# A GDN / short-conv / differential-attention backbone on one core: moving activation tiles that begin off the 64-byte grid

## The chip, the cores and the metric

The kernel runs on one core of one Trainium2 chip. The metric is the device time of one execution in microseconds. Before the change it is 2574.88 us, the median of three runs (2573.0 to 2578.13).

## The reference

Two streams of 256 tokens of width 1024, a context and a latent stream, pass through four layers. A layer is a token mixer and a squared-ReLU MLP, each on a normalised and modulated input and added back through a gate:

```
h = rmsnorm(x) * (1 + scale) + shift      # shift, scale, gate: silu(c) @ ada_w[i] + ada_b[i]
x = x + gate1 * mixer(h)                  # layer 0, 3: gated DeltaNet; 1: short conv; 2: differential attention
x = x + gate2 * (square(relu(h2 @ w1)) @ w2)   # w1 1024 x 4096, w2 4096 x 1024
```

Both streams use the same weights; the last layer computes the latent stream alone after its mixer. The output is the latent stream after a last RMSNorm. All of it is float32, and the result must be that of float32 products.

## The kernel before, in words

**Products.** Activations stand transposed: 128 features on the partitions, 512 token columns (context, then latent) along them, eight such tiles for a width of 1024. A float32 product is made of three products in the fast float32 format (F32R): a weight block W is split into `whi` (rounded) and `wlo` (the rest), an activation tile into a high and a low part, and `prod` (L776) adds whi x high, whi x low and wlo x high into one PSUM bank. In each matmul the 128 x 128 weight block is the stationary operand and the activation tile streams past it as the moving operand; a weight load (PEld in the profile) stands ahead of every matmul and runs while the matmul before it streams. So the order for one k is: load whi, stream high; load whi, stream low; load wlo, stream high.

**Tiles.** `hh0..7` and `hl0..7` (L768, names hh and hl in the profile) are the high and low parts of the modulated input of a mixer or an MLP; `u00..u03`, `u10..u13` (L889, named u) are the two parts of 512 hidden features of the MLP, with two buffers each; `yh`, `yl` and the `y` tiles are the mixers' outputs on their way into the output projection. Weights arrive as `raw` (three buffers, SP's DMA queue, `pump_raw` L453), ACT casts them to `whi` and DVE (in the DeltaNet layers POOL) subtracts to get `wlo`; four pairs are held. The second weight of an MLP's last round is kept in pairs of its own, `whix` and `wlox`.

**Where they stand.** Every tile gets its place in a partition of the SBUF from the pools in order of request. As the program is built, `raw`, `whi`, `wlo`, h and u begin at multiples of 64 bytes. What the prediction uses is the distance in bytes, modulo 256, from the weight block that is loaded during a matmul to the tile that streams in it (a column half of 256 tokens, 1024 bytes on, changes nothing in it):

| moving tile | weight loaded meanwhile | distance mod 256 before |
|---|---|---|
| hh, hl | whi, wlo | 0 |
| u | whi, wlo | 128 |
| u | whix, wlox | 0 |
| yh, yl (layer 1) | whi, wlo | 128 |
| yh, yl (layer 1) | whix, wlox | 0 |
| y (layers 0 and 3) | whi, wlo | 32, in their last round 128 |
| y (layer 2) | whi, wlo | 224 |

**Order.** A recording planner (class `Issue`, L68) writes the order of the instructions of every engine: strands of work with priorities, each operation with a cost, and an estimate of when operands and buffers come free, by eighths of a tile's row (`buckets`, L131). PE's order is then fixed. In an MLP (L875 on) PE does, for each 512 hidden features f, the four blocks of w1 on h (24 matmuls each) and then the eight blocks of w2 on the u of f-1 (12 each): 96 and 96 matmuls that follow each other without other work between. The conv mixer does 20 blocks of 24 one after another. In the DeltaNet and attention mixers the blocks on h are interleaved with the small matmuls and transposes of the heads.

**Modulation rows of the next layer.** During the MLPs of layers 0 to 2 the strand `ada_rows` (L589) makes the 6 x 1024 modulation values of the next layer on DVE: 48 loads of 512 KB (`adat`, four buffers, three fetched ahead) over SP's queue, which carries the weights too, and two dot products (L281) for each.

Of the kernel before, what the change touches and what calls it, by code (L numbers as in the profile page):

```python
# [10 lines left out]
F32 = mybir.dt.float32  # L11
F32R = mybir.dt.float32r
# [8 lines left out]
P = 128  # L21
D = 1024
NCH = D // P
T = 256
TT = 2 * T
# [372 lines left out]
class Net:  # L398
# [3 lines left out]
    MM = 3  # L402
    HP, DHP = -20, -20
    SHARE = 0.7
    RAW = 3
    RINGS = (dict(u=4, kt=2, E=2, qd=1, NT=2, scr=2, Z=3, gate=2, o=3, NY=1),
             dict(u=4, kt=3, E=3, qd=3, NT=3, scr=3, Z=4, gate=4, o=4, NY=1))
# [45 lines left out]
    def pump_raw(self):  # L453
        while self.wraw < len(self.wlist):
            ap, kc, cols = self.wlist[self.wraw]
            if cols < P:
                r = self.I.tile(self.wp, "rawab", [P, kc, cols])
            elif sum(c >= P for _, _, c in self.wlist[self.wsplit:self.wraw]) < self.RAW:
                r = self.I.tile(self.wp, "raw", [P, kc, cols], F32, self.RAW)
            else:  # L460
# [119 lines left out]
    def ada_prio(self):  # L580


        self.ada_task.prio = 900 if self.ada_q < 8 + self.phase * self.SHARE else 5000

# [4 lines left out]
    def ada_rows(self, i, pool, ev):  # L589


        I, todo, raws = self.I, deque(range(48)), deque()
        mod = self.mods[i] = I.tile(self.sp, "mod", [P, 48, 2], F32, 2)
        s = I.tile(pool, "adas", [P, 2, D])
        I.load(s, self.a["cvb"])

        def fetch():
            if todo:
                w = I.tile(pool, "adat", [P, D], F32, 4)
                I.load(w, self.a["ada_wT"][i - 1, todo.popleft()])  # L600
                raws.append(w)

        for _ in range(3):
            fetch()
        for r in range(2):
            yield I.act(s[:, r, :], s[:, r, :], AF.Silu)
        I.table(AF.Exp)
        for m in range(48):
            w = raws.popleft()
            for r in range(2):  # L610
                junk = I.tile(pool, "adaj", [P, D], BF16)
                yield I.dot(mod[:, m, r:r + 1], junk, w, s[:, r, :], self.ada_b[:, i, m:m + 1])
            fetch()
            self.ada_ev[i][m // 2].on = m % 2 == 1
        ev.on = True
# [148 lines left out]
    def norm_start(self, i, which, st, halves=(0, 1)):  # L764
        I = self.I
        h = ([], [])
        for k in range(NCH):
            h[0].append(I.tile(self.sp, f"hh{k}", [P, TT], F32R))  # L768
            h[1].append(I.tile(self.sp, f"hl{k}", [P, TT], F32R))
        st["hev"] = [Event(), Event()]  # L770
        st["h"] = h
        for half in halves:
            I.spawn(self.norm_strand(i, which, st, half, h), 3 + half)
# [101 lines left out]
    def mlp(self, i, t0, st, nst, pl):  # L875
        I = self.I
        halves = [h for h in range(2) if h * T >= t0]
        cols = self.full(t0)
        h = st["h"]
        first = yield from self.joint(pl[0, 0], h, [HALF[x] for x in halves])  # L880
        with self.tc.tile_pool(name=f"mlp{i}", bufs=1) as up:
            us = {}
            self.wpool = up
            ada = Event(i + 1 == self.depth)
            if not ada.on:
                I.spawn(self.ada_rows(i + 1, up, ada), 5000)

            def u_tiles(f):
                us[f] = tuple([I.tile(up, f"u{x}{m}", [P, TT], F32R, 2) for m in range(4)] for x in range(2))  # L889

            def u_fin(f, m, ps):
                yield [lambda: I.slot(up, "r", 2)]
                r = I.tile(up, "r", [P, TT], F32, 2, True)
                u = I.tile(up, "u", [P, TT], F32, 2, True)
                yield I.act(r[:, cols], ps[:, cols], AF.Relu)
                I.rel(ps)
                yield I.act(us[f][0][m][:, cols], r[:, cols], AF.Square)
                yield I.act(u[:, cols], r[:, cols], AF.Square)
                yield I.vtt(us[f][1][m][:, cols], u[:, cols], us[f][0][m][:, cols].bitcast(F32), ALU.subtract)
                I.rel(r, u)  # L900

            nf = FF // 512
            for f in range(nf):
                u_tiles(f)
                if f == 0:
                    yield from self.joint_end(*first, lambda m, ps: I.spawn(u_fin(0, m, ps), 2))
                for m in range(0 if f else 4, 4):
                    yield [self.mm_slot()]
                    ps = self.mm_ps()
                    yield from self.block(pl[0, f][m], h, NCH, cols, ps)  # L910
                    self.done(pl[0, f][m])
                    I.spawn(u_fin(f, m, ps), 2)
                if f:
                    yield from self.proj_rounds(i, pl[1, f - 1], 4, 2, us.pop(f - 1), t0, 40, None)
            if i + 1 < self.depth:
                self.norm_start(i + 1, 0, nst)
            yield from self.proj_rounds(i, pl[1, nf - 1], 4, 2, us.pop(nf - 1), t0, 40, nst)
            self.wpool = None
            yield [ada]
# [890 lines left out]
```

## Time and profile before

| | |
|---|---|
| median of three runs | 2574.88 us |
| the profiled execution, its own time | 2573.83 us |
| its span, first to last instruction | 2572.1 us |
| PE busy | 2508.0 us (98%), 16396 matmuls |
| DVE, ACT, POOL busy | 1846.5 us (72%), 1252.0 us (49%), 389.1 us (15%) |
| granted TensorE clock, mean | 0.991 |

The profile has one line per group of instructions: the line of the kernel, the engine, what is written from what, the count, the busy time and the mean duration. A matmul's duration there runs to the end of its drain, while the next one has long begun: the time that a matmul costs its engine is the distance from its start to the next start, which the timeline gives and which is called the pitch here. Start times are us from the span's first instruction.

### The profile page before, as it was taken

Reading aid. Unit: us, or ns where it says so; the run is one execution under the profiler, and the core shown is the slowest. Engines: PE = TensorE matmul, PEld = TensorE weight load, DVE = VectorE, ACT = ScalarE, POOL = GpSimd, SP = SyncE. Lnnn points to the kernel's source line nnn. Section 1 sums busy time; section 2 is a strip of 40 time slices with the busy share of each in tenths; the row PEclk is TensorE's granted clock in tenths of the full one; section 3 lists DMA queues with packets and bytes.
Section 4 is the critical chain, followed back from the end, with each engine's and each line's share of the span. In section 5 each row is a group of like instructions: output and inputs, shape, how many; then the busy total and the mean of one; then the engine's idle time right before and its main releaser. Section 6 shows DMA issues by size and latency. Waiting matters only on the chain. (4 is left out here: it accounts for less than half of the span.)

```text
span 2572.1 us, 41962 instructions
## 1 busy us (share of the span) xinstructions
PE 2508.0 (98%) x16396; PEld 2090.8 (81%) x16396; DVE 1846.5 (72%) x3481; ACT 1252.0 (49%) x2349; POOL 389.1 (15%) x273
## 2 busy tenths in 40 slices
PE   7999999999999999999999999999999999997998
PEld 3778777888888988988889677888888978897998
DVE  5776776699955644999746666799965687775666
ACT  4665665543333433533243454543333577775554
POOL 0444544200000000000000000000000155463000
PEclk9999999999999999999999999999999999998999
DMA  7222212466634133566432322366634111122564
GB/s 290 91 67 67 91 58 75 156 220 213 220 98 125 60 97 107 197 207 219 148 94 77 95 66 70 115 213 215 210 115 124 51 59 42 50 68 75 172 184 129
DMA packets 91638, 323.30 MB, mean 126 GB/s; under 512 B 10288, under 2 KB 13872, under 8 KB 91056
## 3 DMA queue, kind: packets, MB, share of 16 engines
q1 hardware_dynamic: 91440, 320.62, 38.6%
q8 instruction: 129, 2.11, 0.3%
q14 instruction: 69, 0.57, 0.1%
HBM read 317.44 MB, written 1.05 MB: 124 GB/s over the span
## 5 line engine op out<-in xcount | busy, mean ns | idle before, releaser
L257 ACT CAST whi<-raw 128x1024 fp32r<-128x1024 f32 x380 | 399.5, 1051 | 796.4 <-PE ch L236 423.0
L274 DVE TENSOR_TENSOR wlo<-raw,whi 128x1024 fp32r<-128x1024 f32 x305 | 376.2, 1234 | 228.7 <-ACT whi L257 217.3
L236 PE MATMUL mm<-hh,whi 128*128 128x512 f32 (+1 forms) x1344 | 489.6, 364 | 0.0
L236 PE MATMUL mm<-hh,wlo 128*128 128x512 f32 (+1 forms) x1344 | 488.0, 363 | 0.9 <-DVE wlo L274 0.9
L236 PE MATMUL mm<-hl,whi 128*128 128x512 f32 (+1 forms) x1344 | 487.9, 363 | 0.0
L281 DVE CUSTOM_DVE_ANT_0 adaj<-adat,adas,pack 128x1024 bf16<-128x1024 f32 x288 | 368.7, 1280 | 9.4 <-ACT adas L253 5.7
L236 PE MATMUL ch<-u,whi 128*128 128x512 f32 (+1 forms) x1024 | 287.2, 367 | 0.0
L236 PE MATMUL ch<-hh,whi 128*128 128x512 f32 (+3 forms) x784 | 281.2, 359 | 2.1 <-ACT hh L253 2.1
L236 PE MATMUL ch<-hl,whi 128*128 128x512 f32 (+3 forms) x784 | 280.8, 358 | 0.9 <-DVE hl L277 0.9
L236 PEld LDWEIGHTS mm<-hh,wlo 128*128 128x128 f32 x1344 | 256.1, 191 | 31.2 <-issue 5.2
L236 PE MATMUL ch<-hh,wlo 128*128 128x512 f32 (+3 forms) x784 | 281.1, 359 | 0.0
L236 PEld LDWEIGHTS mm<-hh,whi 128*128 128x128 f32 x1344 | 256.4, 191 | 29.1 <-issue 3.7
L236 PEld LDWEIGHTS mm<-hl,whi 128*128 128x128 f32 x1344 | 256.4, 191 | 27.3 <-issue 3.0
L300 POOL TENSOR_TENSOR wlo<-raw,whi 128x1024 fp32r<-128x1024 f32 x75 | 183.2, 2444 | 220.3 <-ACT whi L257 141.0
L236 PE MATMUL mm<-u,whi 128*128 128x512 f32 (+1 forms) x768 | 215.5, 367 | 0.0
L236 PEld LDWEIGHTS ch<-u,whi 128*128 128x128 f32 x1024 | 183.5, 188 | 34.8
L236 PEld LDWEIGHTS <-Z 128*128 128x128 f16 x3072 | 147.3, 97 | 78.0 <-issue 43.9
L236 PE MATMUL ch<-u,wlo 128*128 128x512 f32 (+1 forms) x512 | 187.7, 367 | 0.0
L236 PE MATMUL ch<-Z 128*128 128x64 f16 (+1 forms) x2816 | 174.6, 199 | 7.7 <-DVE Z L269 3.3
L300 POOL TENSOR_TENSOR qk<-qk,rope 128x512 f32<-128x512 f32 x8 | 14.0, 1750 | 1099.6 <-DMA rt<-qk 1063.6
L277 DVE SCALAR_TENSOR_TENSOR x<-mm,mod,x 128x256 f32<-128x256 f32 x284 | 129.1, 479 | 66.6 <-PE mm L236 66.2
L269 DVE CAST_PREDICATED Z<-lev,ch 128x256 f16<-128x256 uint8 x384 | 144.4, 426 | 42.0 <-PE ch L236 38.8
(257 smaller groups left out, 4559.0 us busy)
## 6 DMA issues: line engine op xcount, KB each, us to landing
raw<-in_mlp_w SPq DMA_DIRECT2D x256, 512.0 KB, 3.6
adat<-in_ada_wT SPq DMA_DIRECT2D x144, 512.0 KB, 4.5
raw<-in_gdn_w_in SPq DMA_DIRECT2D x64, 512.0 KB, 3.6
adaw<-in_ada_w SPq DMA_DIRECT2D x48, 512.0 KB, 4.6
raw<-in_sconv_w_in SPq DMA_DIRECT2D x24, 512.0 KB, 3.6
raw<-in_diff_w_in SPq DMA_DIRECT2D x24, 512.0 KB, 3.8
raw<-in_gdn_w_out SPq DMA_DIRECT2D x16, 512.0 KB, 3.5
raw<-in_sconv_w_out SPq DMA_DIRECT2D x8, 512.0 KB, 3.6
```

Of the source, the lines that this page charges most:

```text
L236: op = Op("PE", c, [out], [lhsT, rhs], lambda: self.nc.tensor.matmul(out, lhsT=lhsT, rhs=rhs, start=start, stop=stop, **k), LAT["PE"])
L257: lambda: self.nc.scalar.copy(out=out, in_=in_), LAT["ACT"])
L269: op = self.vec(self._n(data), 130, [out], [data], lambda: self.nc.vector.copy_predicated(out=out, mask=mask, data=data))
L274: return self.vec(self._n(in0), 68, [out], [in0, in1], lambda: self.nc.vector.tensor_tensor(out=out, in0=in0, in1=in1, op=op))
L277: return self.vec(self._n(in0), 130, [out], [in0, in1, scalar], lambda: self.nc.vector.scalar_tensor_tensor(out=out, in0=in0, scalar=scala ...
L281: return self.vec(self._n(in0), 130, [out, junk], [in0, in1, init], lambda: self.nc.vector.tensor_tensor_reduce(out=junk, in0=in0, in1=in1 ...
L300: lambda: self.nc.gpsimd.tensor_tensor(out=out, in0=in0, in1=in1, op=op))
```

## The change

The eight hh and eight hl tiles and the u tiles become 528 instead of 512 columns long (2112 instead of 2048 bytes), and the 512 columns in use begin at a column offset of their own: 4, 8, 12 or 2 columns (16, 32, 48, 8 bytes) for the h tiles, four tiles each, and 1, 3, 5, 6 (high parts) and 7, 9, 10, 14 columns (low parts) for u, which is 4 to 56 bytes. As the tiles follow each other at 2112 bytes, the distance modulo 256 also turns by 64 from one h tile to the next. In the program as built the sixteen h tiles stand at sixteen different distances modulo 256 from the weights (hh: 16, 144, 32, 160, 48, 176, 8, 136; hl: 80, 208, 96, 224, 112, 240, 72, 200), and the u tiles at 132, 12, 148, 24, 156, 36, 168, 56, their second buffers 64 further on. The y, yh and yl tiles and all weights keep their distances. The planner's eighths of an h tile's row are 66 columns then, so that the two halves of a row share one of them. To make room the loads of the modulation rows have three buffers instead of four.

```diff
--- before.py
+++ after.py
@@ -402,6 +402,7 @@
     MM = 3
     HP, DHP = -20, -20
     SHARE = 0.7
+    UO = (1, 3, 5, 6, 7, 9, 10, 14)
     RAW = 3
     RINGS = (dict(u=4, kt=2, E=2, qd=1, NT=2, scr=2, Z=3, gate=2, o=3, NY=1),
              dict(u=4, kt=3, E=3, qd=3, NT=3, scr=3, Z=4, gate=4, o=4, NY=1))
@@ -596,7 +597,7 @@
 
         def fetch():
             if todo:
-                w = I.tile(pool, "adat", [P, D], F32, 4)
+                w = I.tile(pool, "adat", [P, D], F32, 3)
                 I.load(w, self.a["ada_wT"][i - 1, todo.popleft()])
                 raws.append(w)
 
@@ -765,8 +766,9 @@
         I = self.I
         h = ([], [])
         for k in range(NCH):
-            h[0].append(I.tile(self.sp, f"hh{k}", [P, TT], F32R))
-            h[1].append(I.tile(self.sp, f"hl{k}", [P, TT], F32R))
+            for x in range(2):
+                o = (4, 8, 12, 2)[(2 * k + x) // 4]
+                h[x].append(I.tile(self.sp, f"h{'hl'[x]}{k}", [P, TT + 16], F32R)[:, o:o + TT])
         st["hev"] = [Event(), Event()]
         st["h"] = h
         for half in halves:
@@ -886,7 +888,8 @@
                 I.spawn(self.ada_rows(i + 1, up, ada), 5000)
 
             def u_tiles(f):
-                us[f] = tuple([I.tile(up, f"u{x}{m}", [P, TT], F32R, 2) for m in range(4)] for x in range(2))
+                us[f] = tuple([I.tile(up, f"u{x}{m}", [P, TT + 16], F32R, 2)[:, self.UO[4 * x + m]:self.UO[4 * x + m] + TT]
+                               for m in range(4)] for x in range(2))
 
             def u_fin(f, m, ps):
                 yield [lambda: I.slot(up, "r", 2)]
```

PE's order stays as it was but for two swaps at the first layer's start. What moves are the loads and dot products of the modulation rows. On SP's queue, at the start of the first MLP (adat: modulation rows, raw: weights; in brackets the semaphores an issue waits for), there stand before:

```order
L323 DMA adat_6611<-in_ada_wT 128x1024
L323 DMA adat_6617<-in_ada_wT 128x1024 [waits DMAHW5_49,DMAHW1_49,DVE_49]
L323 DMA adat_6639<-in_ada_wT 128x1024 [waits DMAHW6_49,DMAHW2_49,DVE_49]
L323 DMA raw_6655<-in_mlp_w 128x1024 [waits DMAHW3_49,DVE_49]
L323 DMA raw_6693<-in_mlp_w 128x1024 [waits DMAHW4_49,DVE_49]
L323 DMA raw_6712<-in_mlp_w 128x1024 [waits DVE_49]
L323 DMA adat_6730<-in_ada_wT 128x1024 [waits DMAHW7_49]
L323 DMA raw_6742<-in_mlp_w 128x1024 [waits DMAHW3_49,DVE_49]
```

and now:

```order
L323 DMA adat_6611<-in_ada_wT 128x1024 [waits DMAHW5_49,DVE_49]
L323 DMA adat_6617<-in_ada_wT 128x1024 [waits DMAHW6_49,DMAHW1_49,DVE_49]
L323 DMA adat_6625<-in_ada_wT 128x1024 [waits DMAHW7_49,DMAHW2_49,DVE_49]
L323 DMA raw_6662<-in_mlp_w 128x1024 [waits DMAHW3_49,DVE_49]
L323 DMA adat_6679<-in_ada_wT 128x1024 [waits DMAHW4_49,DMAHW0_49,DVE_49]
L323 DMA raw_6700<-in_mlp_w 128x1024 [waits DVE_49]
L323 DMA raw_6719<-in_mlp_w 128x1024 [waits DVE_49]
L323 DMA raw_6737<-in_mlp_w 128x1024 [waits DMAHW3_49,DVE_49]
```

Each adat load now waits for DVE, and a raw load stands behind it more often: the load that fills a buffer follows the two dot products that have just emptied it, where the fourth buffer had been free for the time of a tile. On DVE, in the same place (ISA adaj: a dot product; wlo: a weight's low part; u: a hidden tile's low part), there stand before:

```order
L274 TENSOR_TENSOR wlo_6632<-raw_6261,whi_6631 128x1024
L281 ISA adaj_6641,mod_6586<-adat_6611,adas_6587,pack_85 128x1024
L281 ISA mod_6586 128x1
L274 TENSOR_TENSOR wlo_6658<-raw_6311,whi_6657 128x1024
L274 TENSOR_TENSOR u_1308_6599<-u_6635,u_1304_6595 128x512
L274 TENSOR_TENSOR wlo_6696<-raw_6349,whi_6695 128x1024
L274 TENSOR_TENSOR u_1309_6600<-u_6651,u_1305_6596 128x512
L281 ISA adaj_6672,mod_6586<-adat_6611,adas_6587,pack_85 128x1024
L281 ISA mod_6586 128x1
```

and now:

```order
L281 ISA adaj_6627,mod_6586<-adat_6611,adas_6587,pack_85 128x1024
L281 ISA mod_6586 128x1
L274 TENSOR_TENSOR wlo_6636<-raw_6261,whi_6635 128x1024
L281 ISA adaj_6646,mod_6586<-adat_6611,adas_6587,pack_85 128x1024
L281 ISA mod_6586 128x1
L274 TENSOR_TENSOR wlo_6665<-raw_6311,whi_6664 128x1024
L274 TENSOR_TENSOR u_1308_6599<-u_6639,u_1304_6595 128x512
L274 TENSOR_TENSOR wlo_6703<-raw_6349,whi_6702 128x1024
L274 TENSOR_TENSOR u_1309_6600<-u_6653,u_1305_6596 128x512
```

One more dot product stands ahead of a weight's low part; the work is the same, and the dot products of a layer keep their number, 96.

## Rows read from the trace of the kernel before

**Rows 1.** The page, parts 1 and 2: busy time, granted clock in 40 slices.
```profile
PE 2508.0 (98%) x16396; PEld 2090.8 (81%) x16396; DVE 1846.5 (72%) x3481; ACT 1252.0 (49%) x2349; POOL 389.1 (15%) x273
...
PEclk9999999999999999999999999999999999998999
```

**Rows 2.** Groups of matmuls by form: line, engine, names, tile, count, busy us, mean ns.
```profile
L236 PE MATMUL mm<-hh,whi 128*128 128x512 f32 x824 | 338.6, 411 | 0.0
...
L236 PE MATMUL ch<-u,whi 128*128 128x512 f32 x768 | 241.2, 395 | 0.0
...
L236 PE MATMUL ch<-hh,whi 128*128 128x512 f32 x536 | 208.9, 390 | 0.0
...
L236 PE MATMUL mm<-u,whi 128*128 128x512 f32 x576 | 180.9, 395 | 0.0
...
L236 PE MATMUL mm<-hh,whi 128*128 128x256 f32 x520 | 151.1, 290 | 0.0
...
L236 PE MATMUL ch<-hh,whi 128*128 128x256 f32 x224 | 64.3, 287 | 2.1 <-ACT hh L253 2.1
...
L236 PE MATMUL ch<-u,whix 128*128 128x256 f32 x280 | 51.9, 285 | 0.0
...
L236 PE MATMUL mm<-u,whix 128*128 128x256 f32 x168 | 30.5, 283 | 0.0
```

**Rows 3.** Timeline of PE in the first MLP: start us, length us, line, names, count.
```profile
562.72 0.39 PE L236 MATMUL mm<-hh,whi 128*128 128x512 f32 x1
...
584.50 0.40 PE L236 MATMUL ch<-u,whi 128*128 128x512 f32 x1
...
606.89 0.39 PE L236 MATMUL ch<-hh,whi 128*128 128x512 f32 x1
```

**Rows 4.** Stretches of one kind of matmul: from:to, length us, PE busy (count), clock, DMA.
```profile
874.62:983.45 108.83, 108.83 (x482) 1.00 0.36 111
998.16:1012.09 13.93, 13.93 (x61) 1.00 0.35 107
1624.74:1630.57 5.83, 5.83 (x27) 1.00 0.29 88
1630.80:1643.94 13.14, 13.14 (x112) 1.00 0.14 41
2400.46:2411.85 11.39, 11.39 (x98) 1.00 0.72 223
2411.85:2423.35 11.50, 11.50 (x98) 1.00 0.59 184
```

**Rows 5.** Timeline of PE at the start of the attention layer.
```profile
1415.36 0.40 PE L236 MATMUL ch<-hh,whi 128*128 128x512 f32 x1
...
1415.59 0.40 PE L236 MATMUL ch<-hl,whi 128*128 128x512 f32 x1
...
1415.83 0.39 PE L236 MATMUL ch<-hh,wlo 128*128 128x512 f32 x1
...
1416.52 0.60 PE L244 MATMUL ch<-ident,qk 128*128 128x128 f32 x4
...
1417.19 0.40 PE L236 MATMUL ch<-hh,whi 128*128 128x512 f32 x1
...
1419.26 0.39 PE L236 MATMUL ch<-hh,whi 128*128 128x512 f32 x1
```

**Rows 6.** Timeline of PE in the first DeltaNet layer.
```profile
119.52 0.38 PE L236 MATMUL ch<-abg,selb 96*128 96x512 bf16 x1
119.74 0.27 PE L236 MATMUL ch<-u 128*128 128x128 f32 x1
```

**Rows 7.** Waits: engine, what waited, for what: us in total, times, longest us.
```profile
ACT whi L257 <- PE ch L236: 423.0, 137, 9.0
...
ACT whi L257 <- PE mm L236: 330.2, 130, 4.5
```

**Rows 8.** The page, parts 5 and 6: the dot products of modulation rows, their loads.
```profile
L281 DVE CUSTOM_DVE_ANT_0 adaj<-adat,adas,pack 128x1024 bf16<-128x1024 f32 x288 | 368.7, 1280 | 9.4 <-ACT adas L253 5.7
...
adat<-in_ada_wT SPq DMA_DIRECT2D x144, 512.0 KB, 4.5
```


## The prediction

> **What bounds the kernel.** First the page: PE is busy 98% of the span, at 90% of the full clock or more in all slices but one [rows 1]. So the time is what PE's instructions cost one after another, and the questions are whether the change moves their pitch (start to next start), and whether it makes PE wait. Next the groups by form, for the counts: of the 512-column matmuls on h there are 824 and 536 in the whi-by-hh groups, and as many for hl and for wlo, 3 x 1360 = 4080; on u 768 and 576, and half as many for wlo, 2016; of 256 columns 3 x (520 + 224) = 2232 on h, and 1.5 x (280 + 168) = 672 on u with whix or wlox [rows 2]; the last MLP adds 7 x 96 = 672 on u with whi. The means there run to the end of the drain and are no pitch. So third the timeline and stretches of one kind of matmul. The counts in the stretches include one or two matmuls that were running when they began (and in one case the one that follows); the divisors here are those that start inside, by the code.
>
> In the first MLP 96 matmuls on h take 584.50 - 562.72 = 21.78 us, 226.9 ns each, and the 96 on u that follow 606.89 - 584.50 = 22.39 us, 233.2 ns [rows 3]: the same form, clock and neighbours, and 6.3 ns apart. The table of distances has h at 0 and u at 128 bytes (mod 256) from the weights that are loaded meanwhile. In the conv mixer, h again: 480 in 108.83 us, 226.7 ns. The yh and yl of that layer, at 128: 60 in 13.93 us, 232.2. The y of the attention layer, at 224, that is 32 bytes off the 64-byte grid: 25 in 5.83 us, 233.2 [rows 4]. So of 512 columns one kind stands out, at 227, and all others lie at 232 to 233. With 256 columns it is the other way round: h at distance 0 takes 11.50 us / 96 = 119.8 ns, u at 128 takes 11.39 / 96 = 118.6, y at 224 takes 13.14 / 111 = 118.4 [rows 4].
>
> h itself is not always at 227. Where other matmuls come between, at the start of the attention layer, five starts take 1416.52 - 1415.36 = 1.16 us, 232 each, and nine after the transposes 1419.26 - 1417.19 = 2.07 us, 230 [rows 5]. I read this as a rhythm: a row of matmuls at one distance, 0, settles after some matmuls into a pitch in which loads and streams hinder each other least at 512 columns (and somewhat more than elsewhere at 256). Why that is so no row shows.
>
> **The change part by part.** Its own part is the distances. Sixteen h tiles at sixteen distances, used in turn, leave no row of matmuls at one distance, and none at 0. I expect h to leave its 227 and to run at what all other distances show.
>
> h, 512 columns. Undisturbed are three MLPs of 7 x 4 blocks of 24, 2016, and the conv mixer's 480; of the 1584 others, among head work, I let 300 be settled. 2800 x (232.2 - 226.8) = +15.1 us. The rest already runs at 230 to 232: nothing.
>
> u, 512 columns. 2016 x (232.2 - 233.2) = -2.0 us: one mixed rhythm for another.
>
> h, 256 columns. 2232 x (118.5 - 119.8) = -2.9 us. u with whix and wlox stands at distance 0 too; at h's pitch, 672 x -1.3 = -0.9 us. u with whi in the last MLP is at 118.6 already: nothing.
>
> The sum is +9.3 us. Bounds of the new pitch, which no row shows for starts of 4 to 28 bytes off the grid: from below the nearest row is the bf16 matmul of 512 columns, 119.74 - 119.52 = 0.22 us [rows 6], half the bytes; at 220 for 512 columns and 110 for 256, h wins 2800 x 6.8 + 1280 x 11 = 33 us, u 2016 x 13.2 = 27, the 256-column ones 2904 x 9.8 + 672 x 8.6 = 34: -94 us. From above the longest regular pitch is the 1415.83 - 1415.59 = 0.24 us among the unsettled ones [rows 5]: 2800 x 13.2 + 1280 x 9 + 2016 x 6.8 = +62 us. I take 232.2 and 118.5 because three kinds of tile at three distances, one of them off the grid, agree within 1 ns.
>
> Three buffers instead of four for the modulation rows. 144 loads of 512 KB land 4.5 us after issue, 288 dot products take 1.28 us each [rows 8]. A load now waits on SP's queue for the dot products that have just been issued, and behind it stand loads of weights, which so come up to 2 x 1.28 = 2.6 us later. What hides it: ACT's cast of a weight block waits for PE to release an old pair 137 + 130 times, 423.0 + 330.2 us in all, 2.8 us a time [rows 7]; in these waits the raw weights lie ready. The dots have slack as well: 48 tiles in the seven rounds of 44.2 us that rows 3 show for an MLP, 309 us, are one in 6.4 us, and a load that is fetched two tiles ahead has 12.8 us for its 4.5. Nothing, then; if the cover were gone, up to 144 x 2.6 us is at stake.
>
> Writes to h and u at odd columns are on ACT (49%) and DVE (72%) [rows 1]; PE's wait for the first h of a block totals 2.1 us in its group [rows 2]. Nothing. The swaps at PE's start trade places of neighbours: nothing.
>
> The profiled execution took 2573.83 us, so 2583.1 by its own time; the median of the three runs lies 1.05 above it: 2584.
>
> **Two rules against the rows.** h and u in rows 3 and two kinds of 256 columns in rows 4 differ by 6.3 and 1.2 ns with nothing to tell them apart but tile and distance. The Trainium skill, "TensorE: Matmul & The Clock Gate", section "Step-by-step: what each phase is for", has it that PE reads the stream and the weights through two independent ports of the SBUF, so that loading the next weights takes nothing from the running matmul. By that rule no distance matters and the time stays at 2575; that is rival C, and the traces disagree, though no row changes the distance alone. The y tile of rows 4, which starts 32 bytes off the grid, runs no slower than u on it. The Trainium skill, "SBUF — State Buffer", section "Specifications (TRN2)", gives the SBUF lines of 16 bytes and a penalty for each step to a new line; by it a start inside a line, which u's eight and four of the h tiles get and y's has not, costs one line more per matmul. That is rival B; no row here shows such a start.
>
> **The rivals.** A: the offsets part the two reads and PE gets faster. For it: 220 is there for half the bytes, and y beats h by 1.4 ns at 256 columns. Against it: u on the grid does the same at 118.6, and y gains nothing at 512. Half of the way to the lower bound is -47 us, 2528; a fifth of it 2556.
>
> B: starts off a 16-byte boundary cost each matmul extra. All 3360 matmuls on u and a quarter of the 6312 on h, 4938; priced with the largest lasting difference in the rows, 6.3 ns, it is 31 us over the forecast, 2615; at half that 2600. It decides if single u tiles show a longer pitch than before. Slower, like the forecast, but another mechanism.
>
> C: no change. Either the pitch doesn't hang on the distance, or the mixed h settles at 228 to 229 and the 256-column gain pays for it: 2800 x 1.5 - 2.0 - 3.8 = -1.6 us, 2573 to 2577.
>
> D: the loads of weights come late. It begins where a weight's cast waits for its DMA instead of for PE; 144 x 1.28 us uncovered would be 2575 + 184, but with 2.8 us of cover at the mean only a few could be late: under 10 us, 2585.
>
> **How the numbers follow.** Within 0.2% (5 us) a measurement of this kernel can't tell a change from none. Chances: the forecast 0.48, of which 0.08 ends within 5 us because h settles near 230; A 0.26, of which 0.01 is too small to see; C 0.13; B 0.11; D 0.02. Faster 0.26 (0.25 of A and a bit of C's edge), same 0.20, slower 0.54. The forecast's own range is 2578 to 2592 (h at 230 to 235). The range for 8 in 10 reaches down over the lesser half of A and up over half of B: 2546 to 2602.
>
> **What would show it.** In the timeline of the first MLP: 96 matmuls on h in 22.2 to 22.4 us instead of 21.78, those on u in 22.2 to 22.5; in the last MLP 96 on h in 11.35 to 11.42 instead of 11.50; the 480 of the conv mixer in 111.4 instead of 108.83; yh, yl and y as before; casts still waiting for PE by over 700 us. The forecast is wrong if the 480 take under 109.5 us, and A is right if both h and u there are under 225 ns; B, if u is over 235.

## The result, and the profile after

The changed kernel takes 2589.86 us, the median of three runs (2588.48 to 2591.48), where the kernel before takes 2574.88: 1.0061 times as long, 95% interval 1.0047 to 1.0075. The forecast was 2584, slower; it was right in its direction and 6 us low. The profiled execution of after took 2588.48 us, 14.65 more than the one of before.

The page of after, busy time and granted clock:

```profile
PE 2523.0 (98%) x16396; PEld 2094.4 (81%) x16396; DVE 1850.3 (72%) x3481; ACT 1252.8 (48%) x2349; POOL 388.5 (15%) x273
...
PEclk9999999999999999999999999999999999998999
```

PE is busy for 15.0 us more than in [rows 1], with as many instructions and the same share of the span; the clock is as it was. So no wait has come in: the same matmuls take longer. Where, the timeline of PE in the first MLP shows (start, length, names, count), in the round of [rows 3]:

```profile
563.23 0.39 PE L236 MATMUL mm<-hh,whi 128*128 128x512 f32 x1
...
585.54 0.40 PE L236 MATMUL ch<-u,whi 128*128 128x512 f32 x1
...
608.00 0.39 PE L236 MATMUL ch<-hh,whi 128*128 128x512 f32 x1
```

The 96 matmuls on h take 585.54 - 563.23 = 22.31 us, 232.4 ns each, where they took 21.78; the 96 on u take 22.46, 234.0 ns, where they took 22.39. Stretches of one kind (from:to, length, PE busy and count, granted clock, DMA share, GB/s), the 480 of the conv mixer, 112 of the attention layer's y, and 96 on u and 96 on h in the last MLP, beside [rows 4]:

```profile
878.56:990.05 111.49, 111.49 (x482) 1.00 0.35 109
1642.16:1655.42 13.26, 13.26 (x114) 1.00 0.13 41
2415.85:2427.30 11.45, 11.45 (x99) 1.00 0.70 223
2427.30:2438.69 11.39, 11.39 (x99) 1.00 0.61 185
```

The 480 went from 108.83 to 111.49 us, 226.7 to 232.3 ns. The y stretch is read one matmul further than in [rows 4] (112 in 13.26 us: 118.4 ns) and is as fast. With 256 columns h fell from 119.8 to 118.6 ns and u rose from 118.6 to 119.3.

What ACT waits for (us in total, times, longest), beside [rows 7]:

```profile
ACT whi L257 <- PE ch L236: 430.0, 138, 8.8
ACT whi L257 <- PE mm L236: 337.6, 130, 4.6
```

and the page of after on the dot products and their loads, beside [rows 8]:

```profile
L281 DVE CUSTOM_DVE_ANT_0 adaj<-adat,adas,pack 128x1024 bf16<-128x1024 f32 x288 | 368.7, 1280 | 9.4 <-ACT adas L253 5.7
...
adat<-in_ada_wT SPq DMA_DIRECT2D x144, 512.0 KB, 4.2
```

The casts of weights still wait for PE, 767.6 us in all, so the weights are still early; the three buffers cost nothing that shows here.

Summed over the whole trace, from the start of each matmul to the next: those on h of 512 columns 1008.8 us before and 1024.2 after (+15.5), on u of 512 columns 470.2 and 471.5 (+1.3), on h of 256 columns 291.1 and 289.0 (-2.2), on u of 256 columns 162.6 and 163.3 (+0.7). That is +15.3; what is left to the 14.65 is in the y, yh and yl rows and the head work, where no kind differs by more than 0.9 us either way.

### The profile page after: what moved, and what is told of

It reads as the page before. It is cut to its first block, busy times and chain, and to the rows that moved or that the text cites. A ratio compares the mean times of both kernels' runs of the same rounds, so it can differ in the third digit from the quotient of the medians.

```text
span 2586.8 us, 42063 instructions
## 1 busy us (share of the span) xinstructions
PE 2523.0 (98%) x16396; PEld 2094.4 (81%) x16396; DVE 1850.3 (72%) x3481; ACT 1252.8 (48%) x2349; POOL 388.5 (15%) x273
```

## The experiments

Theory: the distance (in bytes, modulo 256) between the weights that are loaded and the tile that streams sets the pitch, and h loses because it leaves distance 0. Rivals: the loss is in starts off the 64-byte grid; in the place of the tile itself; in the three buffers. The first kernels take the change apart (their times against the runs of before on the same chip: 2575.12 us for the first four, 2573.48 for the next four, 2575.11 for the ninth, 2574.06 for the last three).

**1. Three buffers alone.**

```
-                w = I.tile(pool, "adat", [P, D], F32, 4)
+                w = I.tile(pool, "adat", [P, D], F32, 3)
```

> Only the loads of the modulation rows go from four to three buffers; all distances are those of before. Theory (the distances of h alone cost the time): as before, 2573 to 2577 us, 96 matmuls on h in the first MLP in 21.78 us, casts of weights waiting for PE by over 700 us. Rival 'buffers' (weights come late behind the waiting loads): most of the 15 us stand here, 2585 to 2590, with PE idle before weights.

Measured 2574.82 us, ratio 0.9999 (0.9990 to 1.0009). The buffers are nothing. All kernels below have three.

**2. The offsets of h alone** (u's tiles as before).

```
+            for x in range(2):
+                o = (4, 8, 12, 2)[(2 * k + x) // 4]
+                h[x].append(I.tile(self.sp, f"h{'hl'[x]}{k}", [P, TT + 16], F32R)[:, o:o + TT])
```

> h as changed (16 distances, 8 to 48 bytes off the grid), three buffers, u as before. Theory: h of 512 columns at 232, u at 233.2, nearly the whole difference: 2586 to 2589 us. Rival 'off the grid' (what costs is that a tile begins beside a multiple of 64 bytes): h and u share the loss by their counts, 4080 to 2016, so about two thirds of the 15 us, 2584 to 2585; rival 'buffers': 2575.

Measured 2587.8 us, ratio 1.0052 (1.0035 to 1.0069). Stretches of the first MLP, 96 on h and then 96 on u:

```profile
563.59:585.89 22.30, 22.30 (x97) 1.00 0.77 240
585.89:608.19 22.30, 22.30 (x98) 1.00 0.66 198
```

h carries nearly the whole loss. And u, untouched at distance 128, went from 22.39 to 22.30 us, over the trace from 233.2 to 232.2 ns: its starts no longer lie 229 and 238 ns apart in turn but go through a longer cycle, from 228 to 241 ns. So its pitch depends a little on what ran before it.

**3. The offsets of u alone** (h as before).

```
+    UO = (1, 3, 5, 6, 7, 9, 10, 14)
+                us[f] = tuple([I.tile(up, f"u{x}{m}", [P, TT + 16], F32R, 2)[:, self.UO[4 * x + m]:self.UO[4 * x + m] + TT]
+                               for m in range(4)] for x in range(2))
```

> u as changed (4 to 56 bytes off the grid, each tile its own distance), three buffers, h as before. Theory: u had no settled low pitch to lose, 233.2 goes to 233.9: plus 1 to 2 us, 2575 to 2578. Rival 'off the grid': a third of the loss, 2579 to 2581, u over 235 ns.

Measured 2576.67 us, ratio 1.0006 (0.9997 to 1.0015). The same two stretches:

```profile
562.04:583.83 21.79, 21.79 (x98) 1.00 0.76 236
583.83:606.28 22.45, 22.45 (x98) 1.00 0.66 201
```

h keeps its pitch (227.0 ns, before 226.9), and u pays some hundredths of a us a block: from start to start the first three MLPs take 0.3 us more each and the last one 0.4, 1.4 us, which the times can hardly tell from nothing.

**4. A map of distances.** All u tiles of a round get one offset, another in each round, so that each row of 96 matmuls has a single distance. The tiles are 576 columns long, 2304 bytes or nine times 256, so all eight stand alike.

```
+    UB = ((0, 4, 8, 12, 16, 20, 24, 16), (28, 32, 36, 40, 48, 56, 64, 64), (80, 96, 112, 128, 144, 160, 192, 128), (0, 4, 8, 16, 32, 64, 128, 32))
+                o = self.UB[i][f] // 4
+                us[f] = tuple([I.tile(up, f"u{x}{m}", [P, TT + 64], F32R, 2)[:, o:o + TT] for m in range(4)] for x in range(2))
```

> h as before; all eight u tiles of one MLP round stand at one distance, another in each round (0 to 192 bytes further than before, so 128 to 255 and 0 to 64 mod 256 from the weights), 96 matmuls at each. Theory (a row of matmuls at one distance settles into a rhythm, and at 512 columns only distance 0 has the short one): 226.7 ns a matmul, 21.8 us for the 96, in the round at 0; 231 to 234 at the distances 128, 160, 192, 224, 32; what starts of 4 to 28 bytes off the grid give at one distance is open, 225 to 238. Rival 'off the grid': the rounds on multiples of 64 bytes (128, 192, 0, 64) are all alike and shorter than all others. Rival 'tile, not distance': all rounds stay at 233.2.

Measured 2572.94 us in one run. Rows of 96 on u at distances 128, 132, 152, 156 and 0 with 512 columns, and 128, 132 and 192 with 256:

```profile
539.65:562.04 22.39, 22.39 (x97) 1.00 0.69 211
583.81:606.84 23.03, 23.03 (x97) 1.00 0.65 198
805.22:827.62 22.40, 22.40 (x97) 1.00 0.62 188
1080.48:1102.24 21.76, 21.76 (x97) 1.00 0.68 203
1832.34:1854.10 21.76, 21.76 (x97) 1.00 0.67 206
2399.96:2411.36 11.40, 11.40 (x99) 1.00 0.67 218
2422.86:2434.62 11.76, 11.76 (x98) 1.00 0.60 178
2515.12:2526.02 10.90, 10.90 (x98) 1.00 0.65 192
```

Four bytes make 6.7 ns: 132 takes 239.9 ns where 128 takes 233.2, and 156 takes 226.7 where 152 takes 233.3. The distance 156 is 28 bytes off the grid, and as fast as h at 0 in the kernel before; u itself reaches 226.7 when it stands at 0. So neither the grid nor the tile decides. The theory missed one thing here: it had distance 0 as the only short one, and 156 is a second. With 256 columns 192 takes 113.5 ns, less than any row of before. (The Trainium skill, "SBUF — State Buffer", section "Specifications (TRN2)", has a penalty for each step to a new line of 16 bytes; the tile at 156 begins 12 bytes into such a line, and no penalty shows.)

**5. h on the grid, but at four distances in turn.** The tiles are 528 columns long, so each stands 64 bytes further on than the last, and no column offset is used.

```
+            for x in range(2):
+                o = 0
+                h[x].append(I.tile(self.sp, f"h{'hl'[x]}{k}", [P, TT + 16], F32R)[:, o:o + TT])
```

> As before, but the h tiles are 528 columns long and h still begins at the first: the sixteen h tiles stand at distances 128, 64, 0 and 192 from their weights in turn, all of them multiples of 64 bytes, with no column offset. Theory (what counts is that h leaves distance 0, where 512 columns run at 226.7 ns; the map of distances gave 229 to 234 at 64, 128 and 192): h of 512 columns at 230 to 233 ns, about +13 us, 2585 to 2589 us. Rival (starts at odd columns, off the 64-byte grid, make the loss): h stays at 226.7, 2575 us.

Measured 2582.56 us in one run; 96 on h and the 480 of the conv mixer:

```profile
563.31:585.50 22.19, 22.19 (x97) 1.00 0.73 230
...
876.97:987.92 110.95, 110.95 (x483) 1.00 0.35 109
```

231.1 ns for both, inside the theory's 230 to 233, with every start on the grid. Summed over the trace h of 512 columns pays 12.9 us. The time is below the expected range because the expectation left out h of 256 columns (-2.6) and u, which again ran faster behind another h (-1.7).

**6. The weights moved by 128 bytes, h and u by 256, which is nothing modulo 256.**

```
+            if n == 0:
+                I.tile(self.wp, "gap0", [P, 32])
```

and the same once more when both rings of weight buffers (four `whi`, four `wlo`) have been requested. In the program as built both rings stand 128 bytes further on, and everything behind them, h and u too, 256.

> As before, but the two rings of weight buffers stand 128 bytes further on, by an unused tile ahead of each; h, u and y stay where they are. So h comes to stand at distance 128 and u at 0: the two change places. Theory (the distance between weights and moving tile sets the pitch): u of 512 columns falls from 233.2 to 226.7 ns (2016 of them, -13 us), h of 512 rises from 226.7 to 233 (2800 settled ones, +18 us), h of 256 columns falls from 119.8 to 118.6 (-2.5), u of 256 in the last MLP rises by as much (+0.8): about 2578 us. Rival (the place of the h and u tiles themselves decides): h stays at 226.7 and u at 233.2, 2575 us.

Measured 2580.9 us in one run. First MLP, h (now at 128) and u (now at 0); last MLP, h at 128 and u at 0:

```profile
563.44:585.83 22.39, 22.39 (x97) 1.00 0.75 235
585.83:607.61 21.78, 21.78 (x97) 1.00 0.64 200
...
2510.90:2522.29 11.39, 11.39 (x98) 1.00 0.62 186
2522.29:2533.79 11.50, 11.50 (x98) 1.00 0.63 184
```

h and u have changed places to the hundredth of a us: 21.78 and 22.39 in [rows 3] are 22.39 and 21.78 here, 11.50 and 11.39 in [rows 4] are 11.39 and 11.50. Over the trace h of 512 columns pays 18.0 us, as expected, and u wins 13.0. It is the distance between the two operands, and nothing of the tiles themselves. (The Trainium skill, "TensorE: Matmul & The Clock Gate", section "Step-by-step: what each phase is for", gives stream and weights two independent ports; by that rule this move costs and gains nothing. The measurement decides against it.) The time is 3 us above the expected 2578; the two DeltaNet layers took 3.6 us more than before, but they did so by 4.8 in the kernel with three buffers alone, so that much is theirs from one execution to the next.

**7. u at distance 0, h as before.** A gap of 128 bytes ahead of all tiles of the pool in the first three MLPs; the kept weights move with u, so u stays at 0 from them.

```
+            if not t0:
+                I.tile(up, "gap", [P, 32])
```

> As before with three modulation buffers, but in the first three MLPs an unused tile of 128 bytes stands ahead of the others, so that u comes to stand at distance 0 instead of 128; nothing else is moved. Theory (distance 0 gives 512 columns 226.7 ns): 2016 matmuls on u by 6.5 ns are 13 us, 2562 us, ratio 0.995. Rival (u's longer pitch comes from what runs between, the evictions and casts that its rounds wait for, and not from the distance): no change, 2575 us.

Measured 2561.85 us, ratio 0.9954 (0.9937 to 0.9971). h and u of the first MLP:

```profile
562.67:584.43 21.76, 21.76 (x98) 1.00 0.74 230
584.43:606.19 21.76, 21.76 (x98) 1.00 0.68 204
```

Both at 226.7 ns, one rhythm through the round; u of 512 columns gains 13.3 us over the trace. The rival, that u waits for something in its rounds, falls.

**8. A second map**, as the fourth with 24 other distances in the first three MLPs and eight in the last. The last round of an MLP runs with the kept weights, so 21 and seven of them show as rows of 96, in the fourth kernel too.

> As the map of distances, with 24 other distances for u of 512 columns (4, 8, 12, 20, 24, 28, 36, 44, 48, 52, 60, 72, 80, 92, 96, 104, 112, 120, 124, 172, 180, 200, 216, 232 bytes, mod 256) and eight for u of 256 columns (64, 80, 96, 176, 184, 200, 208, 224), one for each round of each MLP. Theory (pitch is a function of the distance, with a floor of 226.7 ns at some distances): most at 229 to 235, a few at 226.7, none under 226; of 256 columns between 113 and 123. Rival (there is no floor, other distances give still less, down to 220 at 512 columns as the 512-column matmul of two bytes an element shows): some under 224. Together about 2573 to 2580 us.

Measured 2574.6 us in one run. Distances 4, 28, 60 and 180 with 512 columns, 200 and 208 with 256:

```profile
540.68:563.40 22.72, 22.72 (x98) 1.00 0.67 207
761.74:783.50 21.76, 21.76 (x98) 1.00 0.32 97
1169.65:1191.41 21.76, 21.76 (x97) 1.00 0.67 204
1876.27:1899.12 22.85, 22.85 (x97) 1.00 0.32 96
2516.13:2527.65 11.52, 11.52 (x99) 1.00 0.63 183
2539.17:2550.37 11.20, 11.20 (x99) 1.00 0.49 142
```

Over both maps, 42 distances of 512 columns: 226.7 ns at 0, 28, 60 and 156, nothing below it, 229 to 238 at the others and 240 at 132. There is a floor, as the theory had it, and it is the same 21.76 us with a DMA share of 0.32 as with 0.67. The mean of the maps over the sixteen distances of h in the changed kernel is 233.1 ns; in the conv mixer it runs at 232.3.

The maps hold one order that the theory did not have. By the remainder that the distance leaves modulo 16 (the weights begin at multiples of 64), the eight distances with remainder 12 take 226.7 to 231.7 ns, 229.0 at the mean, and the eight with remainder 4 take 233.4 to 239.9, at the mean 236.2; those with 8 lie at 233.2 to 235.5, and those with 0, without distance 0 itself, at 229.1 to 234.7. Three of the four best distances, 28, 60 and 156, have the remainder 12, and the worst, 132, has 4. Each distance was taken in one row, behind h at 0.

**9. The best distances.** 0 for 512 columns, 192 for 256 where a tile has no matmul of 512. `Back` makes a tile begin some columns earlier; `gapx` stands ahead of the kept weights. The gap of the seventh kernel, and one like it ahead of yh and yl in the conv mixer, belong to it and are left out below.

```
+class Back:
...
+    def __getitem__(self, s):
+        return self.t[s[0], s[1].start - self.n:s[1].stop - self.n]
...
+        if which and i == self.depth - 1:
+            h = tuple([Back(t, 16) for t in x] for x in h)
...
+                if t0:
+                    us[f] = tuple([Back(t, 48) for t in x] for x in us[f])
...
+            if home == "x0" or home == "x4":
+                I.tile(pool, "gapx", [P, 16 if pool.name != f"mlp{self.depth - 1}" else 32])
```

> The distances are now chosen by the maps: 0 for moving tiles of 512 columns (h as before; u of the first three MLPs and the conv mixer's yh and yl by an unused tile of 128 bytes), 192 for those of 256 columns wherever a tile has no columns of 512 (in the last MLP h and u, whose latent half is written 64 and 192 bytes ahead in its own tile; everywhere the weights that are kept for the halves, by an unused tile of 64 or 128 bytes). Theory (pitch is a function of the distance): 2016 on u by 6.6 ns = -13.3 us, 768 on h of the last MLP by 6.4 = -4.9, 672 on u there by 5.2 = -3.5, 672 on u and 192 on y with the kept weights by 6.5 = -5.6, 96 on yh and yl by 6 = -0.6: -28 us, 2547 us, ratio 0.989. Rival (113.4 ns is the best of one row of matmuls on one weight ring, not of the distance): h of the last MLP or u with the kept weights stays at 117 to 120, 2555 to 2562 us.

Measured 2555.48 us (five runs, 2548.66 to 2556.91), ratio 0.9912 (0.9897 to 0.9927): the fastest so far, but 8 us short of the expectation. Stretches: 112 on u with the kept weights at the end of the first MLP, the 80 that follow, then of the last MLP the first 21 on h, and later 96 on h and 96 on u, all at distance 192:

```profile
822.40:835.59 13.19, 13.19 (x113) 1.00 0.14 41
835.84:845.12 9.28, 9.28 (x83) 1.00 0.01 2
...
2360.64:2365.58 4.94, 4.94 (x21) 0.50 0.00 0
...
2487.59:2498.89 11.30, 11.30 (x98) 1.00 0.64 188
2498.89:2510.20 11.31, 11.31 (x99) 1.00 0.63 187
```

The last MLP runs at 11.31 / 96 = 117.8 ns and not at 113.5, and so does the first row (13.19 / 112). After a break of 0.25 us the same u goes on at the same distance; the first of the 80 is held up for 0.31 us from start to start, four take 117 to 122 ns, and the other 75 lie 113.3 ns apart. This repeats: in all three MLPs of this kernel and of the next three the row of 112 runs at 117.8 ns and the row of 80 settles at 113.3. So the rival is right in part: the distance alone doesn't set the pitch at 192. The last three kernels ask what does.

**10. h of the last MLP back at 0** (its two lines with `Back(t, 16)` taken out).

> As the best distances, but h of the last MLP is back at distance 0; u there stays at 192, and nothing else is moved. In the execution profiled of the best distances, h and u of the last MLP ran at 117.8 ns, both at distance 192, with one rhythm from the one to the other; in the map of distances u at 192 ran at 113.3, and h before it at 0. Theory (at 192 there are two rhythms, 117.8 and 113.3 ns, each held as long as the row lasts, and which one it is is set where the row begins, here by h at another distance): u of the last MLP at 113.3 (672 by 4.5 = -3.0 us), h at 119.8 (768 by 2.0 = +1.5), 2554 us against the 2555.5. Rival (113.3 belonged to the longer tiles of the map, whose neighbours stand 2304 bytes apart): u stays at 117.8, 2557 us.

Measured 2556.58 us, ratio 0.9927 (0.9913 to 0.9942). h, then u, in the last MLP:

```profile
2488.93:2500.43 11.50, 11.50 (x98) 1.00 0.63 185
2500.43:2511.33 10.90, 10.90 (x99) 1.00 0.67 192
```

u has not been touched and runs at 113.5 ns instead of 117.8: what ran before it set its rhythm. From its first matmul on h to its first with the kept weights the last MLP takes 171.3 us, 0.9 less than in the ninth kernel's trace. The whole time shows none of it: in this execution the first MLP began 2.8 us later after the first DeltaNet layer, at 495.5 us against 492.7.

**11. h of the last MLP at 208.**

```
-            h = tuple([Back(t, 16) for t in x] for x in h)
+            h = tuple([Back(t, 12) for t in x] for x in h)
```

> As the best distances, with h of the last MLP at 208 (116.65 ns for u in the second map) and u at 192. Theory (pitch by distance, with the rhythm set anew at each change of distance): h 768 by 116.7 - 117.8 = -0.9 us, u 672 by 113.3 - 117.8 = -3.0 us: 2551.5 us. Rival as for the kernel with h at 0: u at 117.8, 2554.6 us.

Measured 2554.11 us (2549.92 to 2555.66), ratio 0.9915 (0.9901 to 0.9930):

```profile
2485.79:2497.23 11.44, 11.44 (x98) 1.00 0.61 185
2497.23:2508.11 10.88, 10.88 (x98) 1.00 0.63 192
```

u at 113.3 again. But h at 208 takes 119.2 ns, where u took 116.7 at that distance: a miss, which costs 1.9 us on the 768 matmuls on h and leaves the time above the 2551.5 expected, and one more case of a distance with two rhythms.

**12. The ninth kernel again**, unchanged.

> The best distances once more, unchanged. Its five times were 2548.66, 2548.76, 2555.48, 2556.81 and 2556.91 us. Theory (two rhythms at distance 192): in the fast executions the last MLP runs at 113.3 ns as a whole, 1440 by 4.5 = 6.5 us, so the times come in two groups some 7 us apart, and the profiled execution shows 113.3 when it is one of the fast group and 117.8 when not. Rival (the spread is that of the kernel before, which also spans 7 us): times spread evenly, and the profile shows 117.8 whatever its time.

Measured 2550.39 us (four runs, 2549.25 to 2552.73), ratio 0.9902 (0.9885 to 0.9919). The first 23 on h, and later 96 on h and 96 on u, in the last MLP:

```profile
2363.08:2368.46 5.38, 5.38 (x23) 0.50 0.00 0
...
2485.59:2496.47 10.88, 10.88 (x98) 1.00 0.63 194
2496.47:2507.35 10.88, 10.88 (x98) 1.00 0.65 193
```

The same program, the same distance, and now 113.3 ns for all rows of the last MLP. From its first matmul on h to its first with the kept weights it takes 166.0 us, where the ninth kernel's trace has 172.2. So 192 has two rhythms with 256 columns, and an execution falls into one or the other where h begins. What chooses is not shown. In both traces PE had stood idle for 2.07 us before h, and the first matmuls on h run at a granted clock of 0.50, the lower of the two levels (1.2 GHz), from the third on 213.3 ns apart; the clock rises to 1.00 during the 22nd matmul in the ninth kernel's trace and the 24th in this one, and within five matmuls of that each has the rhythm that it keeps. The nine times of this program lie at 2548.66 to 2552.73 (six) and 2555.48 to 2556.91 (three), with the profiled ones, one of each rhythm, on the sides that fit; two groups are likely. The gap between them is 2.75 us over both series, but within the ninth kernel's five, on one chip, it is 6.7 (2548.76 to 2555.48), near the 6.1 by which the two traces differ in the last MLP. Only two executions have a trace. This is the version to keep, some 20 to 24 us faster than the kernel before in both series.

## Why the prediction was right

**What bounds the kernel: right.** PE stayed at 98% and the matmuls' pitch made the difference.

**h, 512 columns: right.** Predicted 232.2 ns and +15.1 us; the conv stretch shows 232.3 and the sum over the trace +15.5: 14.2 in the 2496 undisturbed ones (13.5 by the prediction's own figures), 1.3 among head work, where the allowance of 300 settled ones, which no row gave, came to 1.6. The mechanism, h losing its distance 0, is shown by the sixth kernel, which takes h away from 0 without touching it, and by the second, which has the loss without u's offsets. The reading of h as a settled rhythm held as well: in the kernel before, the row of [rows 3] begins with starts 231, 233 and 231 ns apart and goes on at 226 and 227. That the figure came so close is in part luck. The prediction took 232.2 because three kinds of tile at three distances agreed, but u, yh and yl all stood at 128 and y at 224, two distances, and the maps have single ones from 226.7 to 239.9 ns.

**u, 512 columns: wrong in size and sign.** Predicted -2.0 us, measured +1.3. The step that failed is "one mixed rhythm for another": it took 232.2 ns, the value of yh and yl, for every mixture. u before was no mixture but a row at one distance, 128, at 233.2; at its new distances it averages 233.9. The row at 128 can lose those 1 ns (second kernel), but u's own offsets don't do it.

**256 columns: half right.** h: predicted -2.9, measured -2.2; the 96 of the last MLP fell to 11.39 us, inside the 11.35 to 11.42 that were named. u with the kept weights: predicted -0.9, measured +0.3; u of the last MLP: predicted 0, measured +0.4. The same step failed: other distances were priced as equal, and the maps' rows of 96 have them from 113.5 to 122.7 ns.

**Three buffers: right**, by the first kernel.

**The sum.** +9.3 predicted, +15.3 by the terms measured: 0.4 from h of 512 columns, 3.3 from u of 512, 0.7 from h of 256, and 1.6 from u of 256 make the 6.0.

**The rivals.** A, the offsets speed PE up: for this set of distances not, though single distances do so (113.5 against 119.8), which the forecast had no row for. B, starts off a 16-byte boundary cost each matmul extra: no, by distances 28, 60 and 156; the 26 such distances of the maps average 233.0 ns and the 15 others without 0 232.6, though the starts with remainder 4 do run longer (236.2). C, no change: no, 1.0061 with its interval clear of 1.002. D, late weights: no, by the casts' waits. Of the signs named, the 480 in 111.49 us (111.4 foretold), h in 22.31 (22.2 to 22.4) and u in 22.46 (22.2 to 22.5) came as written.

The bounds of the unknown price were too wide: +62 us rested on 0.24 us of an unsettled row, which one distance of 42 reached (239.9 ns), and -94 us on 220 ns, where no row of 512 columns came below 226.7.

## What to carry to other kernels

Where PE is the bound and matmuls in the fast float32 format follow each other in rows, read the pitch from start to start per kind, not the mean length, and look whether kinds of one shape differ: then the distance between the next weights and the streaming tile is a parameter that an unused tile of 128 bytes sets, worth up to 3% of a row's time here. Move operands against each other one row at a time before spreading them: a spread set of distances gets the mean, about 232 ns here, and gives up the best. And where a row can run in two rhythms, one execution's profile doesn't tell what a distance costs.

## What was not expected of the hardware

With a fixed distance a row settles into a rhythm that repeats: 226.67 ns, which at the granted clock of 1.00 (2.4 GHz) is 544 cycles, for 512 columns at 0, 28, 60 and 156, and 113.33 ns, 272 cycles, for 256 at 192. Four bytes more or less move it by up to 6.7 ns, and a remainder of 12 modulo 16 goes with short pitches, one of 4 with long ones. That 256 bytes more or less change nothing is seen at distance 0: with tiles 2048 bytes apart (seventh kernel) and 2304 (fourth) the 96 take 21.76 us. At 192 and 256 columns two rhythms, 113.3 and 117.8 ns, both lasted for as long as the row did, in one case through the 160 us of the last MLP; at 208 there were 116.7 and 119.2, at 104 (second map, kept weights of the third MLP) 120.0 and after a break 129.9, and with 512 columns at 128 233.2 and 232.2. That weight loads and streams hinder each other in reading is the likely cause, since moving either has the same effect (sixth and seventh kernels); no run shows it directly. Why 0, 28, 60 and 156 are good and what picks the rhythm where a distance has two stays open, and so does whether the block being loaded counts or the block in use: within a row both stand at the same distance from the tile.
